# First feed-forward projection of a hybrid decoder: weights stationary against activations stationary

## The chip, the cores and the metric

The kernel runs on one core of a Trainium2 chip. A core has five engines that run their own instruction streams: TensorE (PE in the profile; PEld is its loading of stationary operands), VectorE (DVE), ScalarE (ACT), GpSimd (POOL) and SyncE (SP), which here only issues DMAs. The metric is the device time of one execution in microseconds (us), lower is better.

## The reference, cut to what matters

Two layers, 256 tokens, width 1024. Each layer is a half-step SwiGLU feed-forward network (FFN), a token mixing (windowed attention beside a diagonal state-space model, SSM), and a second FFN. All of it is float32.

```python
D_MODEL, SEQ, DEPTH, D_FF = 1024, 256, 2, 2816

def swiglu(h, w_in, w_out):
    a, b = jnp.split(h @ w_in, 2, axis=-1)
    return (jax.nn.silu(a) * b) @ w_out

for l in range(DEPTH):
    mod = (c_act @ w_ada[l] + b_ada[l]).reshape(Bsz, N_MOD, 1, D_MODEL)
    ...
    x = x + 0.5 * g1 * swiglu(modulate(rmsnorm(x, norm_ffn1[l]), sh1, sc1), w_ffn1_in[l], w_ffn1_out[l])
    x = x + g2 * mixing(modulate(rmsnorm(x, norm_mix[l]), sh2, sc2), ...)
    x = x + 0.5 * g3 * swiglu(modulate(rmsnorm(x, norm_ffn2[l]), sh3, sc3), w_ffn2_in[l], w_ffn2_out[l])
return rmsnorm(x, final_norm)
```

The SSM inside `mixing` needs, for each of 16 tiles of states in a layer, a table of the cosine and sine of the state's angle over the 256 tokens.

## The kernel before

The program is six sublayers in a row: FFN (sublayer 0), mixing (1), FFN (2), FFN (3), mixing (4), FFN (5). Activations lie with features on the 128 partitions and the 256 tokens along the free dimension: 8 chunks of 128 features, each split into a high float32r part (`hh`) and the rest (`hl`).

**Weights.** They arrive from HBM in units of 1 MB (`raw`, four buffers, DMAs issued by SP). Each unit is cut into two halves of 1024 columns. `split_one` splits a half: ACT casts it to `whi` (L163), DVE subtracts to get `wlo` (L164). Seven halves are in flight (`NHB`). `look`, called at each `half()`, splits as far ahead as buffers allow, so that the casts stand in ACT's stream some six halves ahead of the matmuls that read them. Among the weight units come units of the modulation's weights (`wada`), which DVE alone multiplies and sums (`ada_unit`, L247).

**First projection of an FFN** (`ffn_sub`). The 2816 gated columns are 22 tiles of 128; a loop over 11 pairs `p` makes, for each pair, two tiles of `a` (g = 0) and two of `b` (g = 1). A tile is one half of weights: 8 chunks times the three products of `mm3` (L201 to L203), each with a 128x128 block of weights stationary and 256 tokens moving. So a pair is 4 halves and 96 matmuls. Then ACT makes Silu (L843), DVE the product (L845), ACT and DVE split it in two (`split_act`, L340 and L341). The result has features on partitions, as the second projection (`fo`, 8 x 22 tiles) needs it. The first tiles of the stage come from `first_sublayer` (8 tiles, sublayer 0) or `first_block` (6 tiles, elsewhere).

**Tables beside it.** In sublayers 0 and 2, `side` holds a generator `table_side` that makes the 16 tables of the layer. Each `tick()` takes one step of it: first 12 (sublayer 0) or 8 (sublayer 2) empty steps, then 32 real ones, by turns "angles of state tile s" (`tp` and `tq` on ACT, L509 and L510, then four operations on POOL: L389, L387, L392, L392) and "cosine and sine of state tile s - 2" (`tb` on ACT, L525 to L527, then a DMA that POOL issues, L528). `tp` has three buffers, `tq` two, so `tq` of state tile s waits until POOL is done with s - 2, and `tb` of s - 2 waits for the same. The loop over pairs calls `tick` three times in a pair.

**Order.** ACT, POOL and SP run in the order in which the code emits; the order on PE and DVE is made by a scheduler when the kernel is built. Every engine runs its stream in order.

Of the kernel before, what the change touches and what calls it, by code (L numbers as in the profile page):

```python
# [58 lines left out]
NZ = 6  # L59
NATIVE = ()  # L60
# [3 lines left out]
def plan_units():  # L64
    """Order in which the units of weights are read: ('w', i) or ('a', i)."""
# [37 lines left out]
def trunk(ctx, tc, xT, cv, par, ssmp, cst, emat, tbl, wada, wpk, bmat, cmat, out):  # L103
# [37 lines left out]
    def take_ada():  # L141
        """Modulation units whose turn it is."""
# [42 lines left out]
    def several(n):  # L185
        """Halves that are read together."""
# [13 lines left out]
    def mm3(ps, wh, wl, hh, hl, start, stop):  # L200
        T.matmul(ps, lhsT=wh, rhs=hl, start=start, stop=False)  # L201
        T.matmul(ps, lhsT=wh, rhs=hh, start=False, stop=False)  # L202
        T.matmul(ps, lhsT=wl, rhs=hh, start=False, stop=stop)  # L203
# [31 lines left out]
    def ada_unit():  # L235
        """256 columns of silu(c) @ w_ada, one column per partition and element."""
# [57 lines left out]
    def soon(fn):  # L294
        """fn, with its instructions ahead of those that are emitted up to SOON earlier."""
# [16 lines left out]
    def rstd_start():  # L312
        """1 / sqrt(mean of squares + eps), tokens on partitions."""
# [17 lines left out]
    def rstd_spread(ys):  # L331
        """The same on every partition, in PSUM."""
# [10 lines left out]
    def h_tiles(r, scale, shift, hh, hl):  # L343
        """scale * x * r + shift in two parts, chunk by chunk; the chunks take turns in how much of it
        the scalar engine does."""
# [9 lines left out]
        for k in range(KC):  # L355
            hh.append(base.tile([128, S], F32R, name=f"hh{k}", tag=f"hh{k}"))
            hl.append(base.tile([128, S], F32R, name=f"hl{k}", tag=f"hl{k}"))
            b = shift[:, k:k + 1]
            if k % 2:
                A.activation(out=hh[k], in_=t, func=AF.Identity, bias=b)  # L360
            else:
                A.activation(out=t, in_=t, func=AF.Identity, scale=scale[:, k:k + 1], bias=b)
                A.copy(out=hh[k], in_=t)
            n = first(k + 1) if k + 1 < KC else None
            if k % 2:
                stt(hl[k], t, b, hh[k], AD, SU)
            else:
                tt(hl[k], t, hh[k], SU)
# [133 lines left out]
    def table_side(l, pool):  # L502
        """Cosine and sine of each state's angle over time, for the scans of layer l."""
# [27 lines left out]
    def gate_of(sub):  # L531
        """Half the gate."""
# [71 lines left out]
    def first_block(nx, sj, rj):  # L604
        """Five column tiles of a sublayer's input projection. They read scale * x; the rest read the
        normed chunks, which are made meanwhile. What comes back: the banks, 1 / rms, the normed chunks."""
# [5 lines left out]
        def mm(j, w, k):  # L612
            mm3(pss[j][:, :S + 2], w[0][:, k, :], w[1][:, k, :], z[:, k, 0, :], z[:, k, 1, :], k == 0, k == KC - 1)

        hh, hl = [], []
# [13 lines left out]
        for j in range(4):  # L629
            for k in range(5, KC):  # L630
                mm(j, hs[j], k)
            if j == rj:
# [3 lines left out]
                ht = h_tiles(rs, scale, shift, hh, hl)  # L636
# [12 lines left out]
        return pss, rs, hh, hl  # L649

    def first_block_whole(nx, sub):
        """The same for four column tiles, in plain float32."""
        scale, shift, z = nx
        us = [("w", first[sub] + j) for j in range(2)]
        ws = [raw.pop(u).rearrange("p (a b) -> p a b", b=128) for u in us]
        look()
        pss = [bank("b1") for _ in range(4)]

        def mms(ks):
            for j in range(4):  # L660
                for k in ks:
                    T.matmul(pss[j][:, :S + 2], lhsT=ws[j // 2][:, 8 * (j % 2) + k, :], rhs=z[:, k, :],
                             start=k == 0, stop=k == KC - 1)
                if ks[0] == 0 and j == 1:
                    stat_mm()
                    stat["ys"] = rstd_start()
                if ks[0] > 0 and j % 2:
                    finish(us[j // 2])
                    take_ada()

        mms(range(5))
        rps = rstd_spread(stat["ys"])
        rs = tmp.tile([128, S], F32, name="rs", tag="sqa", bufs=1)
        A.copy(out=rs, in_=rps)
        hh, hl = [], []
        for k in h_tiles(rs, scale, shift, hh, hl):
            pass
        mms(range(5, KC))
        look()
        return pss, rs, hh, hl  # L680
# [39 lines left out]
        # bias of each head by distance, for each kind of block of keys: [pq + pk] is that of query  # L720
        # 127 - pq and key pk of the block
# [661 lines left out]
```

## Time and profile before

| | us |
|---|---|
| median of 3 runs (lowest, highest) | 1365.01 (1364.72, 1365.94) |
| span of the profiled execution | 1361.8 |
| PE busy | 1322.1 (97%) |
| DVE busy | 1098.3 (81%) |
| ACT busy | 757.2 (56%) |
| POOL busy | 292.6 (21%) |

The profile is of one execution, whose span runs from its first to its last instruction; what lies around it in that execution is not listed; the median of the three runs is 3.2 us above the span. Matmuls overlap, so that PE's busy share says that it always had one in flight, not that it ran at its peak: how fast it goes is the distance between the starts of two matmuls. Idle time of an engine counts only where PE waits for it.

The first projections stand, in the profiled execution, at 52.8 to 170.3 us (sublayer 0), 528.3 to 636.6 (2), 717.3 to 825.5 (3) and 1180.2 to 1288.4 (5).

### The profile page before, as it was taken

How to read it: one execution, taken by the hardware profiler on the slowest of the kernel's cores; microseconds unless marked ns; L12 is line 12 of the kernel's file. 1: busy time of each engine (PE TensorE's matmuls, PEld its weight loads, DVE VectorE, ACT ScalarE, POOL GpSimd, SP SyncE). 2: the span in 40 equal slices, each digit the busy share in tenths (PEclk: the TensorE clock that was granted, in tenths of full speed). 3: DMA queues.
4: the chain of work that ended last, by engine and by line, in shares of the span. 5: the costliest groups of instructions: out<-in, count | busy, mean ns of one | idle time of the engine just before them, and what ended most of it. 6: DMA issues, size and time to landing. Idle time of an engine off the chain costs nothing.

```text
span 1361.8 us, 26855 instructions
## 1 busy us (share of the span) xinstructions
PE 1322.1 (97%) x11018; PEld 1279.4 (94%) x11018; DVE 1098.3 (81%) x1757; ACT 757.2 (56%) x1162; POOL 292.6 (21%) x356
## 2 busy tenths in 40 slices
PE   4996999999999999999999999999999999999997
PEld 2996999998988999999999999999889999999997
DVE  8866997889899879998769888679889887876552
ACT  5634795645565456677646444454565645654441
POOL 5889691100000000877300000010000000000000
PEclk9997999999999999999999999999999999999999
DMA  9775997556665645998837988656555463586540
GB/s 356 297 289 175 369 347 274 187 193 207 219 234 219 217 153 170 347 370 321 279 124 291 351 316 333 247 174 227 173 199 198 163 220 128 182 307 217 186 155 32
DMA packets 48837, 321.60 MB, mean 236 GB/s; under 512 B 6048, under 2 KB 6432, under 8 KB 12746
## 3 DMA queue, kind: packets, MB, share of 16 engines
q1 hardware_dynamic: 41704, 296.24, 59.8%
q0 software_dynamic: 7008, 23.64, 5.4%
q8 instruction: 86, 1.41, 0.4%
q14 instruction: 37, 0.30, 0.1%
q10 hardware_dynamic: 2, 0.00, 0.0%
HBM read 310.38 MB, written 9.48 MB: 235 GB/s over the span
## 4 chain that ended last, share of the span: by engine, by line
PE 86%; POOL 6%; DVE 3%; issue 2%; ACT 1%; DMA 1%; DVEq 0%; POOLq 0%; ACTq 0%
PE pc L203 8%; PE pc L201 8%; PE pc L202 8%; PE fo L201 6%; PE fo L202 6%; PE fo L203 6%; PE qk L201 4%; PE qk L202 3%; PE qk L203 3%; PE gt L201 3%; PE gt L202 2%; PE gt L203 2%; PE b L201 2%; PE bu L949 2%; PE b L203 2%; PE b L202 2%
## 5 line engine op out<-in xcount | busy, mean ns | idle before, releaser
L164 DVE TENSOR_TENSOR wlo<-raw,whi 128x1024 fp32r<-128x1024 f32 x416 | 515.5, 1257 | 93.2 <-ACT whi L163 92.3
L163 ACT CAST whi<-raw 128x1024 fp32r<-128x1024 f32 x416 | 427.0, 1047 | 220.2 <-PE fo L202 71.3
L201 PE MATMUL pc<-hl,whi 128*128 128x256 f32 x1200 | 338.4, 282 | 8.7 <-ACT whi L163 8.7
L203 PE MATMUL pc<-hh,wlo 128*128 128x256 f32 x1200 | 338.2, 282 | 3.6 <-DVE wlo L164 3.6
L202 PE MATMUL pc<-hh,whi 128*128 128x256 f32 x1200 | 338.2, 282 | 0.0
L201 PEld LDWEIGHTS pc<-hl,whi 128*128 128x128 f32 x1200 | 226.6, 189 | 8.9 <-ACT whi L163 8.9
L203 PEld LDWEIGHTS pc<-hh,wlo 128*128 128x128 f32 x1200 | 226.5, 189 | 4.1 <-DVE wlo L164 4.1
L202 PEld LDWEIGHTS pc<-hh,whi 128*128 128x128 f32 x1200 | 226.7, 189 | 0.0
L201 PE MATMUL fo<-al,whi 128*128 128x256 f32 x704 | 197.7, 281 | 0.2 <-DVE al L341 0.2
L202 PE MATMUL fo<-ah,whi 128*128 128x256 f32 x704 | 197.8, 281 | 0.0
L203 PE MATMUL fo<-ah,wlo 128*128 128x256 f32 x704 | 197.7, 281 | 0.0
L247 DVE CUSTOM_DVE_ANT_0 raw<-raw,cb 128x1024 f32<-128x1024 f32 x144 | 182.2, 1300 | 7.4 <-DMA raw<-wada 7.1
L201 PEld LDWEIGHTS fo<-al,whi 128*128 128x128 f32 x704 | 132.6, 188 | 0.4 <-DVE al L341 0.4
L202 PEld LDWEIGHTS fo<-ah,whi 128*128 128x128 f32 x704 | 132.7, 188 | 0.0
L203 PEld LDWEIGHTS fo<-ah,wlo 128*128 128x128 f32 x704 | 132.7, 188 | 0.0
L201 PE MATMUL qk<-hl,whi 128*128 128x256 f32 x352 | 102.4, 292 | 0.0
L202 PE MATMUL qk<-hh,whi 128*128 128x256 f32 x352 | 99.1, 282 | 0.0
L203 PE MATMUL qk<-hh,wlo 128*128 128x256 f32 x352 | 98.7, 281 | 0.0
L389 POOL TENSOR_SCALAR tr<-tp 128x256 f32<-128x256 f32 x32 | 45.6, 1424 | 146.8 <-ACT tp L509 146.1
L883 POOL DMA_DIRECT2D tab<-tab x32 | 17.4, 545 | 267.8 <-DVE pq L276 171.3
L201 PE MATMUL gt<-hl,whi 128*128 128x256 f32 x256 | 74.7, 292 | 0.0
L201 PEld LDWEIGHTS qk<-hl,whi 128*128 128x128 f32 x352 | 66.1, 188 | 7.1 <-issue 4.7
(220 smaller groups left out, 2915.4 us busy)
## 6 DMA issues: line engine op xcount, KB each, us to landing
raw<-wpk SPq DMA_DIRECT2D x208, 1024.0 KB, 5.4
raw<-wada SPq DMA_DIRECT2D x72, 1024.0 KB, 6.8
tab<-tb POOLq DMA_DIRECT2D x32, 256.0 KB, 5.7
tab<-tab POOLq DMA_DIRECT2D x32, 256.0 KB, 3.6
bt<-wd POOLq DMA_DIRECT2D x8, 640.0 KB, 6.2
xt<-xT SPq DMA_DIRECT2D x1, 1024.0 KB, 4.9
bT<-bmat POOLq DMA_DIRECT2D x2, 512.0 KB, 4.8
out<-xt SPq DMA_DIRECT2D x4, 256.0 KB, 2.2
```

The costliest lines, as they stand in the source:

```text
L163: A.copy(out=hi.rearrange("p a b -> p (a b)"), in_=src)
L164: low.tensor_sub(out=lo.rearrange("p a b -> p (a b)"), in0=src, in1=hi.rearrange("p a b -> p (a b)"))
L201: T.matmul(ps, lhsT=wh, rhs=hl, start=start, stop=False)
L202: T.matmul(ps, lhsT=wh, rhs=hh, start=False, stop=False)
L203: T.matmul(ps, lhsT=wl, rhs=hh, start=False, stop=stop)
L247: V.tensor_tensor_reduce(out=wj, in0=wj, in1=cb, scale=1.0, scalar=0.0, op0=ALU.mult, op1=ALU.add, accum_out=m[:, c:c + 1])
L389: G.tensor_scalar(out=o, in0=i, scalar1=s1, scalar2=s2, op0=op0, op1=op1)
L883: G.dma_start(out=tabs[s], in_=tabd[l][s])
L949: T.matmul(ps[:, i * S:i * S + S], lhsT=w[r, i, q, :], rhs=u[q][r], start=n == 0, stop=n == 2, tile_position=(32 * jj, 0))
```

## The change

In pairs 2 to 10 of each FFN's first projection (the pairs up to `OLD` = 2 stay as they were) the operands change places: a chunk of activations, 128 tokens, is stationary, and 512 columns of weights (two tiles of `a`, two of `b`) move. Result tiles have tokens on the partitions, one bank of PSUM for each half of the tokens. Silu and product are made on 256 columns for each half of the tokens; four PE transposes for a pair turn the product back, and the split reads the transposed product from PSUM. The transposes of a pair are emitted after the next pair's matmuls. The weights are packed on the host so that a half now holds two chunks of all 512 columns. `block512` calls `tick` after each of its four halves, and the loop once more: five calls in a pair. High and low parts of an activation now share a tile (`hx`, `ax`).

```diff
+    def mmt(ps, x, t, wh, wl, start, stop):
+        sl = slice(128 * t, 128 * t + 128)
+        T.matmul(ps, lhsT=x[:, 0, sl], rhs=wh, start=start, stop=False)
+        T.matmul(ps, lhsT=x[:, 1, sl], rhs=wh, start=False, stop=False)
+        T.matmul(ps, lhsT=x[:, 1, sl], rhs=wl, start=False, stop=stop)
+
+    def block512(name, x, n, tock):
+        ps = [bank(name) for t in range(2)]
+        for h in range(n // 2):
+            wh, wl = (w.rearrange("p (a b) c -> p a (b c)", a=2) for w in half())
+            for t in range(2):
+                for k in (2 * h, 2 * h + 1):
+                    mmt(ps[t], x[k], t, wh[:, k % 2], wl[:, k % 2], k == 0, k == n - 1)
+            tock()
+        return ps
...
+        def turned():
+            p, mu = waiting.pop(0)
+            pt = bank("pt").rearrange("p (j s) -> p j s", j=2)
+            for j in range(2):
+                for t in range(2):
+                    T.transpose(pt[:, j, 128 * t:128 * t + 128], mu[:, t, 128 * j:128 * j + 128], ident)
+            split_act(pt, ax[2 * p][0][:, :, 1], ax[2 * p][0][:, :, 0])
+
+        waiting = []
         for p in range(FC // 2):
...
+            if p >= OLD:
+                ps = block512("pc", hx, KC, tick)
+                for t in range(2):
+                    A.activation(out=sl[:, t], in_=ps[t][:, :S], func=AF.Silu)
+                    V.tensor_mul(out=mu[:, t], in0=sl[:, t], in1=ps[t][:, S:])
+                if waiting:
+                    turned()
+                waiting.append((p, mu))
+                tick()
+                continue
             for g in range(2):
...
-                    ps, rough = column(q, j, p < FC // 2 - 1 or g == 0)
+                    ps, rough = column(q, j, True)
...
             tick()
-            split_act(flat(mu), flat(a), flat(b))
+            split_act(mu, a[:, :, 1], a[:, :, 0])
+        turned()
...
     def ffn(w_in, w_out):
         t = tiles(w_in)
         for p in range(FC // 2):
-            for half in range(2):
-                for j in range(2):
-                    cols(t, half * FC + 2 * p + j)
+            if p < OLD:
+                for half in range(2):
+                    for j in range(2):
+                        cols(t, half * FC + 2 * p + j)
+            else:
+                for k in range(KC):
+                    for half in range(2):
+                        seq.append(t[k, half * FC + 2 * p:half * FC + 2 * p + 2])
```

The order on two engines, at the places that the prediction speaks of. ACT in sublayer 0 of the kernel before, from the Silu of pair 4 (`sl_1056`) over the first six steps of the tables (`tp`, `tq` of three state tiles) to the next cast (`whi` are casts of weights, `ah4` is the split of pair 4):

```order
L843 ACTIVATE sl_1056<-pc_1060 128x512
L509 ACTIVATE tp_1124<-cs_71,fhi_97 128x256
L510 ACTIVATE tq_1125<-cs_71,flo_98 128x256
L163 CAST whi_1134<-raw_1023 128x1024
L163 CAST whi_1162<-raw_1023 128x1024
L509 ACTIVATE tp_1197<-cs_71,fhi_97 128x256
L510 ACTIVATE tq_1198<-cs_71,flo_98 128x256
L509 ACTIVATE tp_1206<-cs_71,fhi_97 128x256
L510 ACTIVATE tq_1207<-cs_71,flo_98 128x256
L340 CAST ah4_1058<-mu_1057 128x512
L163 CAST whi_1222<-raw_1093 128x1024
```

The same place of the kernel after, where the tables begin behind the Silu of pair 2 (`sl_765`) and the Silu of pair 3 is `sl_862`:

```order
L840 ACTIVATE sl_765<-pc_769 128x256
L164 CAST whi_867<-raw_778 128x1024
L164 CAST whi_883<-raw_778 128x1024
L543 ACTIVATE tp_906<-cs_71,fhi_97 128x256
L544 ACTIVATE tq_907<-cs_71,flo_98 128x256
L164 CAST whi_915<-raw_810 128x1024
L543 ACTIVATE tp_931<-cs_71,fhi_97 128x256
L544 ACTIVATE tq_932<-cs_71,flo_98 128x256
L164 CAST whi_940<-raw_810 128x1024
L543 ACTIVATE tp_962<-cs_71,fhi_97 128x256
L544 ACTIVATE tq_963<-cs_71,flo_98 128x256
L840 ACTIVATE sl_862<-pc_865 128x256
```

The third `tq`, the first that needs a buffer back from POOL, stood behind the 26th half of weights (`whi_1162`) and stands behind the 22nd (`whi_940`) now, and a Silu is the next thing behind it.

PE in the kernel after, at the end of pair 4's matmuls (`pc_991`); `pt_1100` are the transposes of pair 3's product `mu_863`, `pc_1119` is pair 5:

```order
L217 MATMUL pc_991<-wlo_884,hx7_531 128x512
L828 MATMUL pt_1100<-cs_71,mu_863 128x128 x4
L215 MATMUL pc_1119<-whi_915,hx0_283 128x512
L216 MATMUL pc_1119<-whi_915,hx0_283 128x512
L217 MATMUL pc_1119<-wlo_916,hx0_283 128x512
```

In the kernel before no matmul of a first projection read a Silu; now the matmuls of pair 5 stand behind transposes that need the Silu of pair 3 and its product.

ACT in the kernel after, sublayer 0, from the last step of the tables (`tb_1692`) over the Silu of pair 9 (`sl_1620`) to that of pair 10 (`sl_1726`):

```order
L561 ACTIVATE tb_1692<-tb_1692,cpi_94 128x512
L164 CAST whi_1697<-raw_1577 128x1024
L840 ACTIVATE sl_1620<-pc_1623 128x256
L840 ACTIVATE sl_1620<-pc_1624 128x256
L371 CAST ax8_1493<-pt_1719 128x2x256
L164 CAST whi_1731<-raw_1581 128x1024
L164 CAST whi_1747<-raw_1581 128x1024
L164 CAST whi_1765<-raw_1650 128x1024
L164 CAST whi_1781<-raw_1650 128x1024
L840 ACTIVATE sl_1726<-pc_1729 128x256
L840 ACTIVATE sl_1726<-pc_1730 128x256
```

In the kernel before, the last steps of the tables stood among the casts of the second projection; now all of them stand ahead of the Silu of pair 9.

## Rows read from the trace of the kernel before

**Rows 1.** Page, engines: busy us, share of the span, instructions.

```profile
PE 1322.1 (97%) x11018; PEld 1279.4 (94%) x11018; DVE 1098.3 (81%) x1757; ACT 757.2 (56%) x1162; POOL 292.6 (21%) x356
```

**Rows 2.** Engines by stretch: PE, PEld, DVE, ACT, POOL busy (instructions); clock, DMA, GB/s.

```profile
53.00:170.00 117.00, 104.63 (x862) 103.93 (x862) 89.75 (x109) 64.40 (x100) 97.28 (x141) 0.94 0.73 270
528.00:636.00 108.00, 108.00 (x913) 108.00 (x912) 104.02 (x129) 79.17 (x127) 70.99 (x60) 1.00 0.89 333
717.00:825.00 108.00, 108.00 (x912) 108.00 (x911) 93.83 (x134) 51.65 (x62) 0.00 (x0) 1.00 0.85 319
1180.00:1288.00 108.00, 108.00 (x912) 108.00 (x912) 73.78 (x93) 53.74 (x66) 0.00 (x0) 1.00 0.67 243
```

**Rows 3.** PE in order of time: start us, us, instruction, idle before it.

```profile
112.99 0.58 PE L201 MATMUL pc<-hl,whi 128*128 128x256 f32 x1 [8.73 <-ACT whi L163]
...
117.43 0.58 PE L203 MATMUL pc<-hh,wlo 128*128 128x256 f32 x1 [3.64 <-DVE wlo L164]
...
118.24 0.41 PE L203 MATMUL pc<-hh,wlo 128*128 128x256 f32 x1
118.45 0.41 PE L201 MATMUL pc<-hl,whi 128*128 128x256 f32 x1
...
170.29 0.28 PE L201 MATMUL fo<-al,whi 128*128 128x256 f32 x1
...
636.55 0.28 PE L201 MATMUL fo<-al,whi 128*128 128x256 f32 x1
```

**Rows 4.** ACT by line, 53 to 170 us: instructions, busy, mean ns, idle before.

```profile
L163 ACT CAST whi<-raw 128x1024 fp32r<-128x1024 f32 x36 | 35.8, 1045 | 7.1 <-DMA raw<-wpk 5.9 <-PE pc L202 1.0
L527 ACT ACTIVATE tb<-tb,cpi 128x512 f32<-128x512 f32 x8 | 5.8, 725 | 0.3
L510 ACT ACTIVATE tq<-cs,flo 128x256 f32<-128x256 f32 x10 | 5.0, 498 | 24.8 <-POOL tp L392 20.1 <-POOL flo L387 4.7
L526 ACT ACTIVATE tb<-tp,cpi 128x256 f32<-128x256 f32 x8 | 4.0, 496 | 0.0
L525 ACT ACTIVATE tb<-tp 128x256 f32<-128x256 f32 x8 | 3.2, 406 | 0.0
```

**Rows 5.** POOL in order of time: a state tile's four operations and its DMA issue.

```profile
107.30 1.10 POOL L389 TENSOR_SCALAR tr<-tp 128x256 f32<-128x256 f32 x1
110.91 1.08 POOL L389 TENSOR_SCALAR tr<-tp 128x256 f32<-128x256 f32 x1
...
178.89 1.53 POOL L389 TENSOR_SCALAR tr<-tp 128x256 f32<-128x256 f32 x1
184.36 0.61 POOL L528 DMA_DIRECT2D tab<-tb  x1
185.00 1.44 POOL L389 TENSOR_SCALAR tr<-tp 128x256 f32<-128x256 f32 x1
...
547.41 1.28 POOL L389 TENSOR_SCALAR tr<-tp 128x256 f32<-128x256 f32 x1 [126.42 <-ACT tp L509]
```

**Rows 6.** Engines by stretch, columns as in rows 2.

```profile
70.00:93.00 23.00, 23.00 (x196) 23.00 (x195) 18.80 (x25) 9.80 (x14) 20.70 (x31) 1.00 0.83 309
93.00:107.00 14.00, 11.26 (x95) 11.05 (x94) 1.32 (x4) 0.00 (x0) 11.17 (x41) 1.00 0.39 151
118.00:170.00 52.00, 52.00 (x428) 51.81 (x427) 49.64 (x58) 35.21 (x60) 39.90 (x37) 0.97 0.93 347
```

**Rows 7.** PE in order of time, mixing: four transposes of 128 columns, one matmul behind.

```profile
389.07 0.60 PE L1050 MATMUL pt<-cs,lg 128*128 128x128 f32 x4
389.43 0.37 PE L201 MATMUL gt<-hl,whi 128*128 128x256 f32 x1
389.64 0.60 PE L1050 MATMUL pt<-cs,lg 128*128 128x128 f32 x4
```

**Rows 8.** DVE by line, 118 to 170 us, columns as in rows 4.

```profile
L164 DVE TENSOR_TENSOR wlo<-raw,whi 128x1024 fp32r<-128x1024 f32 x18 | 24.7, 1401 | 0.9 <-ACT whi L163 0.9
L247 DVE CUSTOM_DVE_ANT_0 raw<-raw,cb 128x1024 f32<-128x1024 f32 x14 | 20.0, 1466 | 0.0
```

More of the change, by code (lines that the diff above doesn't have):

```diff
@@ L59 @@
 NZ = 6
+OLD = 2
 NATIVE = ()
@@ L198, in wtile, with mm3, mm2, mmz @@
         return cur[0][0][:, k, :], cur[0][1][:, k, :]
[L200 to L203, printed above, removed]
+    def mm3(ps, wh, wl, x, start, stop):
+        T.matmul(ps, lhsT=wh, rhs=x[:, 0], start=start, stop=False)
+        T.matmul(ps, lhsT=wh, rhs=x[:, 1], start=False, stop=False)
+        T.matmul(ps, lhsT=wl, rhs=x[:, 1], start=False, stop=stop)
+    def mm2(ps, wh, wl, x, start, stop):
+        T.matmul(ps, lhsT=wh, rhs=x.rearrange("p a b -> p (a b)"), start=start, stop=False)
+        T.matmul(ps[:, :S], lhsT=wl, rhs=x[:, 1], start=False, stop=stop)
+    def mmt(ps, x, t, wh, wl, start, stop):
[12 more added lines that the diff above has]
+        return ps
+    def mmz(ps, wh, wl, z, start, stop):
+        T.matmul(ps, lhsT=wh, rhs=z[:, 1], start=start, stop=False)
+        T.matmul(ps, lhsT=wh, rhs=z[:, 0], start=False, stop=False)
+        T.matmul(ps, lhsT=wl, rhs=z[:, 0], start=False, stop=stop)
     cs = base.tile([128, 385], F32, name="cs")
@@ L341, in split_act, with part_tile, h_tiles @@
         V.tensor_sub(out=lo, in0=src, in1=hi)
-    def h_tiles(r, scale, shift, hh, hl):
+    def part_tile(k):
+        return base.tile([128, 2, S], F32R, name=f"hx{k}", tag=f"hx{k}")
+    def h_tiles(r, scale, shift, hx):
         def first(k):
@@ L648, in first_block @@
             split_one()
[L649 to L680, printed above, removed]
+        return pss, rs, hx
     def first_sublayer():
@@ L730, in first_sublayer @@
         pss = [bank("b1") for _ in range(BOOT)]
-        hh, hl, late = [], [], []
+        hx, late = [], []
         def low():
             if late:
-                hl.append(base.tile([128, S], F32R, name=f"hl{len(hl)}", tag=f"hl{len(hl)}"))
-                tt(hl[-1], late.pop(0), hh[len(hl) - 1], SU)
+                x, t = late.pop(0)
+                tt(x[:, 0], t, x[:, 1], SU)
         def mms(k):
             for j in range(BOOT):
-                T.matmul(pss[j][:, :S], lhsT=hs[j][0][:, k, :], rhs=hh[k], start=k == 0, stop=False)
-                T.matmul(pss[j][:, :S], lhsT=hs[j][1][:, k, :], rhs=hh[k], start=False, stop=False)
+                T.matmul(pss[j][:, :S], lhsT=hs[j][0][:, k, :], rhs=hx[k][:, 1], start=k == 0, stop=False)
+                T.matmul(pss[j][:, :S], lhsT=hs[j][1][:, k, :], rhs=hx[k][:, 1], start=False, stop=False)
             for j in range(BOOT):
-                T.matmul(pss[j][:, :S], lhsT=hs[j][0][:, k, :], rhs=hl[k], start=False, stop=k == KC - 1)
+                T.matmul(pss[j][:, :S], lhsT=hs[j][0][:, k, :], rhs=hx[k][:, 0], start=False, stop=k == KC - 1)
         for k in range(KC):
@@ L753, in first_sublayer @@
             t = boot.tile([128, S], F32, name="hb", tag="hb", bufs=2)
-            a = base.tile([128, S], F32R, name=f"hh{k}", tag=f"hh{k}")
+            hx.append(part_tile(k))
             A.activation(out=t, in_=xr[:, k, :], func=AF.Identity, scale=sc[:, k:k + 1], bias=sh[:, k:k + 1])
-            A.copy(out=a, in_=t)
-            hh.append(a)
-            late.append(t)
+            A.copy(out=hx[k][:, 1], in_=t)
+            late.append((hx[k], t))
             if k == 0:
@@ L822, in ffn_sub @@
             mu = fp.tile([128, 2, S], F32, name="mu", tag="mu", bufs=2)
-            a = fp.tile([128, 2, S], F32R, name=f"ah{p}")
-            b = fp.tile([128, 2, S], F32R, name=f"al{p}")
+            a = fp.tile([128, 2, 2, S], F32R, name=f"ax{p}")
+            ax += [(a, a[:, 0]), (a, a[:, 1])]
+            if p >= OLD:
[8 more added lines that the diff above has]
+                continue
             for g in range(2):
@@ L847, in ffn_sub @@
             tick()
-            split_act(flat(mu), flat(a), flat(b))
-            ah += [a[:, 0], a[:, 1]]
-            al += [b[:, 0], b[:, 1]]
+            split_act(mu, a[:, :, 1], a[:, :, 0])
+        turned()
+        ax = [x for _, x in ax]
         gate = gate_of(sub)
@@ L947, in ssm_in @@
                 for i in range(2):
-                    for n, (w, u) in enumerate(((bh, ul), (bh, uh), (bl, uh))):
-                        T.matmul(ps[:, i * S:i * S + S], lhsT=w[r, i, q, :], rhs=u[q][r], start=n == 0, stop=n == 2,
+                    for n, (w, u) in enumerate(((bh, 0), (bh, 1), (bl, 1))):
+                        T.matmul(ps[:, i * S:i * S + S], lhsT=w[r, i, q, :], rhs=ux[q][r, u], start=n == 0, stop=n == 2,
                                  tile_position=(32 * jj, 0))
@@ L1112, in v_quad @@
                             sl = slice(128 * tt_, 128 * tt_ + 128)
-                            T.matmul(o, lhsT=hl[k][:, sl], rhs=wh, start=k == 0, stop=False)
-                            T.matmul(o, lhsT=hh[k][:, sl], rhs=wh, start=False, stop=False)
-                            T.matmul(o, lhsT=hh[k][:, sl], rhs=wl, start=False, stop=k == KC - 1)
+                            T.matmul(o, lhsT=hx[k][:, 0, sl], rhs=wh, start=k == 0, stop=False)
+                            T.matmul(o, lhsT=hx[k][:, 1, sl], rhs=wh, start=False, stop=False)
+                            T.matmul(o, lhsT=hx[k][:, 1, sl], rhs=wl, start=False, stop=k == KC - 1)
                         tock()
```

81 lines of the change are left out of this document (37 added, 44 removed).

## The prediction

> **What bounds the kernel now.** I read the page's table of engines first, then the busy times by stretch, then the order of time around every gap of PE. The engines: PE is busy 97% of the span, so what is to be won is won in the pace of its matmuls, and what is to be lost is a wait that PE does not have yet [rows 1]. The stretches: in the first projections of sublayers 2, 3 and 5 PE never rests, 912 or 913 matmuls in 108 us, which is 118.4 ns from start to start [rows 2]. Sublayer 0 is the exception: 104.63 of 117 us, with POOL busy 97.28 [rows 2]. In order of time, PE stands there for 8.73 us until 112.99 because no cast comes from ACT, and 3.64 us more until 117.43 [rows 3]. The waits by line say why ACT was late: `tq` waited 20.1 us for POOL's last operation on a table and 4.7 us for `flo`, a parameter that POOL computes [rows 4]. POOL, still busy with the SSM's parameters, starts its first table at 107.30 [rows 5]. So the thing to look at beside PE's pace is the chain POOL, ACT, PE: ACT runs its stream in order, and a table step that waits for POOL holds up every cast and every Silu behind it.
>
> **The change part by part.**
>
> *Matmuls.* A pair loses 96 matmuls of 256 columns, 96 x 0.1184 = 11.37 us, and gets 48 of 512. No row has a 512-column float32r matmul. Upper bound: twice the 256-column one, 0.237. Lower bound: at half the clock the 256 columns are 0.21 us apart (118.24 to 118.45) [rows 3]; that is the columns alone, since twice as many columns at full clock take the same 0.21, so the lower bound is 0.213. The 12 ns by which the 256-column matmul at full clock (0.1184) exceeds half of that do not show once a matmul lasts 0.21 us. I take 0.215, next to the lower row: 48 x 0.215 = 10.32.
>
> *Transposes.* Four in a pair. In the mixing four of them and one matmul take 389.07 to 389.64, 0.57 us [rows 7]; less 0.12 for the matmul, 0.45. The Trainium skill, page "TensorE: Matmul & The Clock Gate", section "Part 4: PE-mode transpose", gives about 275 ns for one in a kernel's context. The trace disagrees: 0.11 us each in a row of four. By the page's figure a pair would pay 1.1 us instead of 0.45, and the change could not gain on PE at all (estimate: 36 pairs x 0.65 = 23 us, spread over four sublayers, half of it hidden under the waits below).
>
> *PE's balance.* 11.37 - 10.32 - 0.45 = 0.60 us for a pair, 5.4 us for the nine pairs of a sublayer. The last pair's turn was covered before by 20 of 22 tiles of the second projection; now its first transpose stands ahead of that projection. Half of the tokens is finished six matmuls (1.3 us) before the other, and its Silu and product take some 0.4 us each (ACT's 256-column passes take 0.41 to 0.50 [rows 4]), so this wait is short: 0 to 3 us, I take 1. The extra fixed cost of two Silus and two products on ACT and DVE lies under 10.8 us of PE, where DVE has 14 to 34 us free in a stage and ACT more (the last two of [rows 2]). Sublayers 3 and 5, which have no tables: -4.4 each, -9 together. Bounds: 0.237 for the matmul makes a pair 0.45 slower, +4 + 1 each, +10.
>
> *Ticks.* This is the part that decides. The tables take 32 steps in either kernel, but the loop calls five in a pair instead of three. A state tile is two steps: 1.5 state tiles in a pair before, 2.5 now. So ACT asks POOL for one in 10.77 / 2.5 = 4.3 us. POOL needs 178.89 to 185.00 = 6.1 us for one while DVE is busy, and 107.30 to 110.91 = 3.6, with 0.61 for the DMA issue 4.2, while DVE rests [rows 5]. Before, the demand was one in 11.37 / 1.5 = 7.6 us, so POOL kept up. Now it does not, and behind the waiting `tq` and `tb` ACT's stream holds casts and Silus, and behind the Silu of pair p PE's stream holds the transposes of p and all of pair p + 2 (the order in the part on the change). The casts run ahead, but PE can't pass the transposes: its lead on ACT is one pair.
>
> How long is a state tile then? DVE works 49.64 us in 52 [rows 6], in which PE ran 428 matmuls or 4.5 pairs: 11 us for a pair. At 2.5 x 5.7 = 14.25 us for a pair DVE is 77% busy, and 4.2 + 0.77 x (6.1 - 4.2) = 5.7: consistent. I take 5.7, bounds 4.2 and 6.2. Half the clock, which PE shows after its waits in the stage now (0.21 us apart until some 3 us after 117.43 [rows 3]), would take its 1 to 2 us out of the 3.5 us that PE then waits in each pair.
>
> *Sublayer 0.* The third `tq` comes four halves earlier and waits for POOL's parameters as before. From then on no casts come, so DVE rests and POOL is quicker: it did 31 operations in 20.7 busy us at 70 to 93 and 41 in 11.17 at 93 to 107, when DVE worked 1.32 us [rows 6]. Before, ACT stopped 20.1 us ahead of 110.91, at 90.8 [rows 4, 5]; now it stops some eight us (three halves of PE's time, which free its buffers) behind pair 2, whose matmuls run from 52.8 to about 64, at 72, so that some 27 of those 31 take 0.27 instead of 0.67: 10 us sooner, the first table at 97.5. Sixteen state tiles x 5.7 = 91 later, at 188.5, POOL is done; ACT makes the last cosine and sine, 0.41 + 0.50 + 0.73, a cast of 1.05 and the Silus of pair 9: 192. Then four casts (4.2), the Silus of pair 10, its product and transposes, some 2 us more: the second projection starts at about 198 instead of 170.29 [rows 3, 4]. +28; at 5.2 and 6.2 us for a state tile +20 and +36.
>
> *Sublayer 2.* The first step lies in pair 2 as before, so POOL starts at 547.41 again [rows 5]; 16 x 5.7 brings it to 638.6. The last step stands ahead of the Silu of pair 8: +3.1 as above, product and transposes 0.9, then pair 10's matmuls, 10.3, and the tail of 2: 655 instead of 636.55 [rows 3]. +19; at 5.2 and 6.2 +11 and +27.
>
> *The rest.* Packing, joint tiles for high and low parts and the first blocks leave the same instructions, DMAs and queues: 0.
>
> **Sum.** 28 + 19 - 9 = +38 on the span of 1361.8 makes 1399.8; with the 3.2 us between span and median, 1403.
>
> **The rivals.**
>
> *The tables hide (ends faster).* If POOL makes a state tile in 4.3 us or less, it never holds ACT. For it: 4.2 us while DVE rests, and that the split of a pair now reads PSUM and not two tiles of SBUF. Against it: DVE has as much to do as before. Then sublayer 0: PE goes on at about 101.5 with six pairs of 10.77 and loses 2 us to half the clock and the tail, 168 against 170.3, so -2; sublayer 2 -4.4; 1365 - 2 - 4.4 - 9 = 1350. The point from which this decides is a state tile of about 4.7 us.
>
> *512 columns cost twice 256.* The tables bind as forecast, and sublayers 3 and 5 cost 10 instead of gaining 9: 1403 + 19 = 1422. For it: the 12 ns might be paid for each 256 columns; against it the spacing at half clock [rows 3].
>
> *POOL and DVE exclude each other wholly.* If POOL's work can't overlap DVE's passes over two operands in SBUF, a pair costs their sum: `wlo` and `ada`, 24.7 + 20.0 us for 4.5 pairs [rows 8], 9.9 for a pair, and 2.5 x 3.4 for POOL, 18.4 in all, 7.4 for a state tile. Sublayers 0 and 2 then cost 27 more each: 1457. Against it: at 118 to 170 POOL made eight state tiles, 27 us of quiet work, beside those 44.7, together more than the 52 there are. It is the rule of the Trainium skill, page "SBUF — State Buffer", section "SBUF: two separate sides", that the pair of ports that these two share is locked for a whole instruction. The trace agrees in kind, since POOL's operations stretch while DVE works, and not in size.
>
> **How the numbers follow.** Forecast 0.67, hidden tables 0.08, 512 at twice the price 0.18, full exclusion 0.07. The forecast's own range is 1387 to 1419 (5.2 to 6.2 us for a state tile). The range for 8 in 10 leaves out most of the first and last rival: 1374 to 1436. About 0.2% is what a measurement of this kernel tells from no change. Faster 0.08, from the first rival; same 0.02, from a state tile near 4.7 us; slower 0.90.
>
> **What would show it.** In sublayers 3 and 5, matmuls of 512 columns 0.215 us apart and the second projection starting some 4 us sooner after the first block. In 0 and 2, POOL without a gap through its 16 state tiles, ACT waiting before `tq` or `tb` for POOL's last operation in nearly each, PE waiting before each `pt` of a pair for the product, and tables that end before the second projection starts. I am wrong if PE's first projections in 0 and 2 stay without such waits, or if POOL's state tiles come 4.3 us apart.

## The result, and the profile after

The changed kernel takes 1427.26 us (1425.62 to 1428.89, four runs) against 1364.87 (1363.96 to 1365.94): a ratio of 1.0455, 95% interval 1.0441 to 1.047. The forecast was 1403, its own range 1387 to 1419, the range for 8 in 10 1374 to 1436. So the sign and the wide range held; the time lies 8 us above the forecast's own range, and the forecast came out 24 us short.

The page's engines after, against [rows 1]: 1584 matmuls fewer and PE at 94% instead of 97% of a span that is 62.7 us longer.

```profile
PE 1344.1 (94%) x9434; PEld 1216.1 (85%) x9434; DVE 1095.2 (77%) x1793; ACT 763.1 (54%) x1198; POOL 282.7 (20%) x356
```

The first projections of sublayers 0, 2, 3 and 5, one row each (columns as in [rows 2]):

```profile
53.00:202.00 149.00, 113.88 (x468) 89.31 (x466) 100.20 (x122) 86.28 (x152) 126.36 (x176) 0.88 0.68 246
562.00:694.00 132.00, 114.78 (x513) 92.14 (x513) 105.56 (x139) 89.84 (x155) 89.63 (x80) 0.95 0.80 288
776.00:885.00 109.00, 109.00 (x510) 89.78 (x509) 96.28 (x143) 54.37 (x71) 0.00 (x0) 1.00 0.84 321
1240.00:1350.00 110.00, 110.00 (x518) 90.69 (x517) 76.77 (x105) 57.54 (x76) 0.00 (x0) 1.00 0.65 238
```

PE rests 35 us in sublayer 0 and 17 in sublayer 2, where it had rested 12 and 0, and the mean granted clock there is lower, 0.88 and 0.95 instead of 0.94 and 1.00. Where there are no tables (sublayers 3 and 5) PE never rests, and the stage is still 1.5 and 1.3 us longer than before. The third number of the lines below is the longest wait; the first three are of 53 to 203 us, the other two of 562 to 695, in the waits by line:

```profile
PE pt L828 <- DVE mu L841: 35.2, 7, 17.1
ACT tb L559 <- DMA tab<-tb: 25.5, 10, 6.0
ACT tq L544 <- POOL tp L426: 21.8, 2, 20.1
...
ACT tb L559 <- DMA tab<-tb: 27.7, 10, 5.8
...
PE pt L828 <- DVE mu L841: 15.9, 4, 6.0
```

PE waits at the transposes, as the order said it must. One of its waits in sublayer 0, the 17.1 us that end at 104.45, is for the first tables; the other 18 us come later. ACT waits for POOL's first tables and, in 20 waits at `tb`, for the DMA that carries off a finished table. POOL in order of time is what [rows 5] were before: it starts its first table at 99.49 and ends its last operation at 189.2, 5.6 us for each of 16 state tiles; in sublayer 2, which begins 34 us later now, at 579.99 and 672.3, 5.8 each. In the first stretch no gap between two of its instructions, DMA issues included, is over 0.1 us until 188.4, nor in the second until 671.2. So POOL sets the pace of the tables, although ACT's waits mostly end with a DMA: POOL issues these DMAs too, behind the operations of a later state tile.

```profile
99.49 1.10 POOL L423 TENSOR_SCALAR tr<-tp 128x256 f32<-128x256 f32 x1
103.10 1.08 POOL L423 TENSOR_SCALAR tr<-tp 128x256 f32<-128x256 f32 x1
107.58 2.06 POOL L423 TENSOR_SCALAR tr<-tp 128x256 f32<-128x256 f32 x1
...
184.68 1.97 POOL L423 TENSOR_SCALAR tr<-tp 128x256 f32<-128x256 f32 x1
...
188.49 0.73 POOL L426 TENSOR_TENSOR tp<-tp,tq 128x256 f32<-128x256 f32 x1
...
579.99 1.23 POOL L423 TENSOR_SCALAR tr<-tp 128x256 f32<-128x256 f32 x1 [125.57 <-ACT tp L543]
```

PE in sublayer 3, a quiet stretch: 512-column matmuls 0.23 us apart, then a pair's transposes.

```profile
802.84 0.40 PE L216 MATMUL pc<-whi,hx 128*128 128x512 f32 x1
803.07 0.39 PE L217 MATMUL pc<-wlo,hx 128*128 128x512 f32 x1
803.30 0.39 PE L215 MATMUL pc<-whi,hx 128*128 128x512 f32 x1
803.53 0.39 PE L216 MATMUL pc<-whi,hx 128*128 128x512 f32 x1
803.76 0.39 PE L217 MATMUL pc<-wlo,hx 128*128 128x512 f32 x1
803.99 0.60 PE L828 MATMUL pt<-cs,mu 128*128 128x128 f32 x4
804.35 0.48 PE L215 MATMUL pc<-whi,hx 128*128 128x512 f32 x1
```

Over the 415 intervals between neighbours in the stage the mean is 0.2322; most lie between 0.228 and 0.233, one in eight between 0.240 and 0.242. (The first interval behind a pair's transposes is often 0.316; it counts to the transposes.)

### The profile page after: what moved, and what is told of

Its sections match the earlier page's. It is cut to its first block, busy times and chain, and to the rows that moved or that the text cites. A ratio compares the mean times of both kernels' runs of the same rounds, so it can differ in the third digit from the quotient of the medians.

```text
span 1424.5 us, 23802 instructions
## 1 busy us (share of the span) xinstructions
PE 1344.1 (94%) x9434; PEld 1216.1 (85%) x9434; DVE 1095.2 (77%) x1793; ACT 763.1 (54%) x1198; POOL 282.7 (20%) x356
## 4 chain that ended last, share of the span: by engine, by line
PE 76%; POOL 17%; DMA 2%; DVE 2%; issue 2%; ACT 1%; POOLq 0%; DVEq 0%; ACTq 0%
PE fo L204 6%; PE fo L203 6%; PE fo L205 6%; POOL tp L426 5%; PE pc L216 5%; PE pc L215 5%; PE pc L217 5%; PE qk L203 3%; POOL tr L423 3%; PE qk L204 3%; PE qk L205 3%; PE gt L203 2%; POOL tr L421 2%; PE gt L204 2%; PE gt L205 2%; PE bu L969 2%
## 5 line engine op out<-in xcount | busy, mean ns | idle before, releaser
L215 PE MATMUL pc<-whi,hx 128*128 128x512 f32 x576 | 233.9, 406 | 0.0
L216 PE MATMUL pc<-whi,hx 128*128 128x512 f32 x576 | 231.7, 402 | 0.0
L217 PE MATMUL pc<-wlo,hx 128*128 128x512 f32 x576 | 227.0, 401 | 1.9 <-DVE wlo L165 1.9
L203 PE MATMUL fo<-ax,whi 128*128 128x256 f32 x704 | 199.3, 283 | 0.0
L204 PE MATMUL fo<-ax,whi 128*128 128x256 f32 x704 | 198.8, 282 | 0.0
L205 PE MATMUL fo<-ax,wlo 128*128 128x256 f32 x704 | 198.7, 282 | 0.0
L217 PEld LDWEIGHTS pc<-wlo,hx 128*128 128x128 f32 x576 | 110.9, 193 | 28.7 <-DVE wlo L165 3.2
L203 PEld LDWEIGHTS fo<-ax,whi 128*128 128x128 f32 x704 | 133.8, 190 | 0.0
L204 PEld LDWEIGHTS fo<-ax,whi 128*128 128x128 f32 x704 | 133.7, 190 | 0.0
L205 PEld LDWEIGHTS fo<-ax,wlo 128*128 128x128 f32 x704 | 133.6, 190 | 0.0
L215 PEld LDWEIGHTS pc<-whi,hx 128*128 128x128 f32 x576 | 111.8, 194 | 24.9 <-ACT whi L164 0.4
L216 PEld LDWEIGHTS pc<-whi,hx 128*128 128x128 f32 x576 | 111.0, 193 | 24.0
L203 PE MATMUL qk<-hx,whi 128*128 128x256 f32 x352 | 102.4, 292 | 0.0
L204 PE MATMUL qk<-hx,whi 128*128 128x256 f32 x352 | 99.1, 282 | 0.0
L203 PE MATMUL gt<-hx,whi 128*128 128x256 f32 x256 | 74.7, 292 | 0.0
L204 PE MATMUL gt<-hx,whi 128*128 128x256 f32 x256 | 72.2, 282 | 0.0
```

What stands on the lines that cost most here:

```text
L203: T.matmul(ps, lhsT=wh, rhs=x[:, 0], start=start, stop=False)
L204: T.matmul(ps, lhsT=wh, rhs=x[:, 1], start=False, stop=False)
L205: T.matmul(ps, lhsT=wl, rhs=x[:, 1], start=False, stop=stop)
L215: T.matmul(ps, lhsT=x[:, 0, sl], rhs=wh, start=start, stop=False)
L216: T.matmul(ps, lhsT=x[:, 1, sl], rhs=wh, start=False, stop=False)
L217: T.matmul(ps, lhsT=x[:, 1, sl], rhs=wl, start=False, stop=stop)
```

## The experiments

All times from the first matmul of a first projection to the first of the second one, in the profiled executions, us:

| kernel | median | sublayer 0 | 2 | 3 | 5 |
|---|---|---|---|---|---|
| before | 1364.9 to 1365.6 | 117.5 | 108.2 | 108.2 | 108.2 |
| after | 1427.3 | 149.4 | 132.3 | 109.7 | 109.6 |
| after, three steps | 1378.1 | 123.9 | 109.7 | 109.7 | 109.6 |
| before, five steps | 1411.2 | 140.5 | 123.7 | 108.2 | 108.2 |
| after, not turned | 1401.3 | 141.0 | 124.4 | 106.1 | 106.1 |
| after, three steps, not turned | 1360.0 | 113.8 | 106.1 | 106.1 | 106.1 |
| after, short POOL | 1391.6 | 131.4 | 114.7 | 109.7 | 109.6 |
| before, tables 4 steps later | 1357.4 | 113.1 | 108.2 | 108.2 | 108.2 |
| after, three steps, tables 4 later | 1371.8 | 118.1 | 109.7 | 109.7 | 109.6 |
| before, tables 10 later | 1351.5 | 102.5 | 108.2 | 108.2 | 108.2 |
| after, three steps, tables 10 later | 1362.3 | 108.6 | 109.7 | 109.7 | 109.6 |

The theory: the loss is the tables' pace, five steps in a pair. The rival: it is the transposes, which tie PE to the Silus. The figures behind a time are its ratio to the kernel before and the ratio's 95% interval.

**Three steps in the changed kernel.**

```diff
-            tock()
+            if h % 2:
+                tock()
```

> The changed kernel with three table steps in a pair instead of five (after the second half, after the fourth, and at the end of the pair). Theory, the pace of the tables: the loss of sublayers 0 and 2 goes, what is left is the longer matmul, about 0.2 us for each of nine pairs in four sublayers, so 1365 + 4 x 1.5 = 1371, at most 1378 with waits for the transposes; the second projections of sublayers 0 and 2 start within 6 us of where they started before. Rival, the transposes themselves: PE cannot pass them, so a late Silu costs PE time whatever the number of steps; the time stays above 1405.

1378.13 (1.0092, 1.0078 to 1.0106): 49 of the 62 us come back, sublayer 2 entirely but for 1.5, what sublayers 3 and 5 lose too. The time lies just above the theory's upper end, because sublayer 0 keeps 6.4 where 6 were allowed: PE waits there 7.3 us for a cast, since ACT waits 19.2 us for the first tables behind POOL's parameters as before, and 7.2 for products. In sublayer 0 fewer steps also move the first table, to 106.84 us, so the pace alone shows in sublayer 2, where POOL starts 18.8 us into the stage and started 17.4 us into it with five steps.

```profile
ACT tq L545 <- POOL tp L427: 19.2, 1, 19.2
...
PE pc L215 <- ACT whi L164: 7.3, 1, 7.3
PE pt L829 <- DVE mu L842: 7.2, 2, 3.6
```

**Five steps in the kernel before.** The other way about: the suspected cost alone, with no change of operands.

```diff
                 for j in range(2):
                     ps, rough = column(q, j, ...)
+                    if p >= 2:
+                        tick()
...
-                tick()
+                if p < 2:
+                    tick()
```

> The kernel before with five table steps in a pair instead of three, nothing else (weights stationary, no transposes). Theory, the pace of the tables: ACT's stream stops behind POOL and with it the casts, so sublayers 0 and 2 get slower by 15 to 30 us each: 1395 to 1425. Rival, the transposes: without them PE runs on over the waits of ACT, 1365 to 1372.

1411.23 (1.0342, 1.0327 to 1.0358): the theory. Without any transposes PE stands all the same, now in front of the weights. The waits of 53 to 194 us, ACT's first:

```profile
ACT tb L525 <- DMA tab<-tb: 25.3, 9, 4.2
...
ACT tq L510 <- POOL tp L392: 21.1, 2, 19.8
...
PE pc L201 <- ACT whi L163: 16.2, 2, 13.9
...
PE pc L203 <- DVE wlo L164: 13.5, 5, 5.0
```

**The changed kernel without the transposes,** with five and with three steps; the operands are changed as before.

```diff
-            pt = bank("pt").rearrange(...)
-            for j in range(2):
-                for t in range(2):
-                    T.transpose(...)
-            split_act(pt, ...)
+            split_act(mu, ...)
```

> The changed kernel, five table steps, without the four transposes of a pair: the split reads the product as it lies, tokens on partitions, so the output is another one. PE then reads no Silu in a first projection. Theory, the pace of the tables with the transposes as an addition: the kernel before with five steps lost 46 us without them, and 48 matmuls of 0.232 are 0.22 us shorter than 96 of 0.1184, 8 us less in all: about 1403 (1398 to 1410), the rest of the changed kernel's loss being the transposes, 16 us of their own time and 5 to 8 of waits. Rival, ACT's order alone (a Silu or cast held by a table step) makes the whole loss and the transposes only add their own time: 1427 - 16 = 1411 or more.

> The changed kernel with three table steps in a pair and without the transposes (the product is not turned, so the output is another one). What is left of the change is the operands alone. Theory: 36 pairs x 0.44 us of transposes and the waits in front of them go, 1378 - 16 - 5 = 1357 (1354 to 1361); sublayers 3 and 5 go from 109.6 us to 106, two below the kernel before. Rival, the transposes lie in time that PE loses anyway: 1375 or more, sublayers 3 and 5 at 109.

1401.31 (1.0266, 1.0251 to 1.0281) and 1359.99 (0.9964, 0.995 to 0.9978): the theory both times. With five steps sublayers 0 and 2 take nearly the same as the kernel before with five steps (141.0 and 124.4 against 140.5 and 123.7). With three steps sublayers 3 and 5, where PE never rests, show the prices: the operands alone gain 2.2 us in a sublayer, and the transposes take back 3.5 or 3.6 there and 0.4 in the second projection: 4.0 for nine pairs, 0.45 us a pair. With five steps the transposes cost 1427 - 1401 = 26 us in all, so the waits that they add to the tables' are 26 - 4 x 4.0 = some 10 us, against the 5 to 8 expected. PE's stretch of sublayer 3 without transposes:

```profile
715.00:820.00 105.00, 105.00 (x476) 86.14 (x475) 93.50 (x138) 53.58 (x71) 0.00 (x0) 1.00 0.86 327
```

48 of the 476 matmuls are of 256 columns (two tiles of pair 1) and take 5.7 us; the other 428 have 99.3, 0.232 each, the same as with transposes.

**POOL's operations on 64 columns.**

```diff
-            gts(b, p, -0.125, AD, MAGIC, AD)
+            n = slice(0, 64)
+            gts(b[:, n], p[:, n], -0.125, AD, MAGIC, AD)
...
```

> The changed kernel, five steps, with POOL's four operations of a state tile on 64 of 256 columns (the tables' other columns stay unreduced, so the output is another one); ACT's steps and the DMAs stay. Theory, POOL's pace: a state tile takes under 3 us, less than the 4.3 that five steps ask for, and the loss of sublayers 0 and 2 goes as with three steps: 1372 to 1384. Rival, what holds ACT is the number of steps in its own stream, or the DMA that frees the tables' buffers: 1410 or more.

1391.57 (1.0189, 1.0173 to 1.0205) lies between the two, in neither range. 36 of the 62 us go, so POOL's pace is the larger part of the loss. But sublayer 2 stays 5 us longer than with three steps. There POOL no longer works without a gap (its gaps add up to 10 us between 561 and 637), and ACT still waits for the tables' DMA, half as long as before (544 to 659 us):

```profile
ACT tb L560 <- DMA tab<-tb: 14.0, 6, 4.7
```

So a second limit seems to stand behind POOL: two buffers for finished tables, and 5 to 7 us from issue to landing; no run gives five steps a third buffer, which would show it. The first line is of the page after, the second of this kernel:

```profile
tab<-tb POOLq DMA_DIRECT2D x32, 256.0 KB, 5.3
```

```profile
tab<-tb POOLq DMA_DIRECT2D x32, 256.0 KB, 6.7
```

The operations did not become four times shorter either. Two of one kind, one behind the other, take 0.33 and 1.35 us here, a spread like that of the SSM's small operations (last section):

```profile
605.98 0.33 POOL L426 TENSOR_TENSOR tp<-tp,tr 128x64 f32<-128x64 f32 x1
606.39 1.35 POOL L426 TENSOR_TENSOR tp<-tp,tq 128x64 f32<-128x64 f32 x1
```

**Tables later in sublayer 0.** The kernel before lost 8.7 and 3.6 us there already [rows 3]; this asks what each kernel is worth without that wait.

```diff
-            side.extend([None] * (12 if sub == 0 else 8) + ...)
+            side.extend([None] * (16 if sub == 0 else 8) + ...)
```

> The kernel before with sublayer 0's tables starting four steps later (16 empty steps instead of 12), so that ACT does not reach the first table step before POOL is done with its parameters. Theory: the waits of 8.7 and 3.6 us and the stretch at half the clock behind them go, 1365 - 12 = 1353 (1350 to 1358). Rival: the last tables move into the second projection and hold its casts, or POOL becomes free later as DVE goes on working beside it: 1362 to 1372.

> The changed kernel with three table steps in a pair and sublayer 0's tables starting four steps later: both disturbances taken out, what is left is the change of operands alone. Theory, the 512-column matmul costs 0.232 us: some 1.5 us more in each of four sublayers than the kernel before with later tables, about 1359 if that one gives 1353. Rival, the change of operands pays in itself once the tables are out of the way: 4 us less for each sublayer, 16 less than that kernel, about 1337.

1357.43 (0.9947, 0.9934 to 0.9959) and 1371.76 (1.0046, 1.0033 to 1.0059). The first lies in the theory's range, with part of its rival's mechanism: DVE goes on beside POOL, and the parameters are done at 118.24 instead of 107.30, so ACT still waits 16.62 us at its third `tq`, and later 8.51 for a table's DMA. In the kernel before with later tables:

```profile
104.82 0.50 ACT L509 ACTIVATE tp<-cs,fhi 128x256 f32<-128x256 f32 x1
121.94 0.51 ACT L510 ACTIVATE tq<-cs,flo 128x256 f32<-128x256 f32 x1 [16.62 <-POOL tp L392]
...
143.04 0.42 ACT L525 ACTIVATE tb<-tp 128x256 f32<-128x256 f32 x1 [8.51 <-DMA tab<-tb]
```

The second kernel came out 14.3 above the first where I expected 6; neither the theory's 1359 nor the rival's 1337. Its sublayer 0 takes 5.0 more, with PE 5.39, 0.80 and 5.28 us in front of transposes, and 2.1 more in the second projection. So the transposes do have a price in waits of their own, in sublayer 0.

**Later still, and a third buffer,** with three table steps instead of two for each tile of the second projection.

```diff
-                tab = pool.tile([128, 2, S], F32, name="tb", tag="tb", bufs=2)
+                tab = pool.tile([128, 2, S], F32, name="tb", tag="tb", bufs=3)
...
-            side.extend([None] * (12 if sub == 0 else 8) + ...)
+            side.extend([None] * (22 if sub == 0 else 8) + ...)
...
-                if k % 8 == 7:
+                if k % 7 == 6:
                     tick()
```

> The kernel before with sublayer 0's tables starting ten steps later (22 empty steps), three steps instead of two for each tile of the second projection so that they end with it, and a third buffer for a finished table. With four steps later ACT still waited for the parameters until 121.94 and 8.51 us for a table's DMA, and PE lost 2.07, 0.76, 3.0 and 0.8 us and half the clock behind them. Theory: these waits go too, sublayer 0's first projection takes the 108.3 us of the other three, 1357.4 - 5 = 1352.5 (1351 to 1355). Rival: the tables now hold the casts of the second projection of sublayer 0, where POOL has as much to do, 1358 to 1366.

> The changed kernel with all that helped the kernel before: three table steps in a pair, sublayer 0's tables ten steps later (22 empty steps), three steps for each tile of the second projection, a third buffer for a finished table. Theory, the change of operands with its transposes costs some 1.4 us in a first projection and 0.5 in the second projection behind it, in each of four sublayers, once no table holds it: 1351.5 + 8 = 1359 (1357 to 1362), a little below the kernel before and above the same kernel with weights stationary. Rival, the transposes meet waits in sublayer 0 in any case: 1364 or more.

1351.53 (0.9905, 0.9889 to 0.992) and 1362.30 (0.9976, 0.9966 to 0.9985), the latter a hair above the theory's range. The kernel before is the fastest of all with this: sublayer 0's first projection has no gap any more and full clock. Its 102.5 us, less than the 108.3 expected, are 864 matmuls at the others' pace; the other three stages have 912. What each of the three edits gave was not told apart.

```profile
53.00:155.00 102.00, 102.00 (x862) 102.00 (x862) 88.48 (x112) 57.22 (x80) 93.65 (x117) 1.00 0.83 308
```

The changed kernel with the same help stays 10.8 us behind it. 4.3 of them are one wait in front of the last pair's transposes, whose product stands in DVE's stream behind four subtractions and a modulation unit. PE, and DVE before it, in that kernel:

```profile
161.19 0.33 PE L829 MATMUL pt<-cs,mu 128*128 128x128 f32 x1 [4.28 <-DVE mu L842]
```

```profile
151.20 5.79 DVE L165 TENSOR_TENSOR wlo<-raw,whi 128x1024 fp32r<-128x1024 f32 x4
157.86 1.60 DVE L279 CUSTOM_DVE_ANT_0 raw<-raw,cb 128x1024 f32<-128x1024 f32 x1 [0.86 <-DMA raw<-wada]
...
159.39 1.40 DVE L279 CUSTOM_DVE_ANT_0 raw<-raw,cb 128x1024 f32<-128x1024 f32 x1
160.72 0.74 DVE L842 TENSOR_TENSOR mu<-sl,pc 128x256 f32<-128x256 f32 x2
```

The rest is 1.3 to 1.8 in a first projection and 0.4 in a second, four times: the change of operands with its transposes as such.

**What 512 columns cost.** Three kernels do none of the kernel's work: groups of matmuls, alone or with other engines and loads beside them, one execution each.

> Matmuls alone, in nine groups of 96 behind 40 to warm up, with all other engines and the DMAs at rest: float32r of 512 columns with the stationary operand changed each time, changed once in 48, and with the same moving operand; float32r of 256 columns with the stationary operand changed each time and once in 48; bfloat16 of 512 and of 256 columns; float32r of 128 and of 384 columns. None of the kernel's work is done. Theory, the price is the matmul's own and linear in its columns: 0.232 us for 512, 0.1185 for 256, 0.175 for 384, with changed and unchanged stationary operand alike. Rival, the change of the stationary operand costs: with an unchanged one 0.213 to 0.216. Rival, the other engines and DMAs slow it in the full kernel: 0.213 to 0.216 in all groups of 512. Rival, float32r: bfloat16 gives 0.213 to 0.216, float32r 0.232.

> Float32r matmuls of 512 columns in groups of 120, each with other company: alone, beside VectorE's subtractions of 1024 columns, beside ScalarE's copies of 1024 columns, beside loads of 1 MB from HBM, beside all three; then 240 of 256 columns beside all three, and 120 of 512 alone again. None of the kernel's work is done. Alone they were 0.2267 us apart in the run of spacings before, in the kernel 0.2322. Theory, company: one of the three, the loads most likely, brings 0.2267 to 0.232, and the 256 columns stay near 0.119. Rival, the kernel's own operands and stream (instructions, semaphores): 0.2267 in every group.

> Float32r matmuls of 512 columns with the changed kernel's own tiles and order (three products, weights in seven high and seven low tiles, activations in eight tiles of two parts, chains of 24 into changing banks), without readers of the banks and then with ScalarE reading them; then one of the three at a time: the activations' tiles as stationary operand, the high tiles as moving operand, high and low tiles by turns as moving operand; at last the kernel before's three products of 256 columns. None of the kernel's work is done. Theory, the kernel's operands: 0.232 us in the first groups, and one of the three single ones shows which, 256 columns at 0.1185. Rival, the kernel's stream (semaphores of many tiles, the other engines' work on the same tiles): 0.2267 in all, 256 columns at 0.120.

The rows by line, with first and last start. In the first run: 512 columns of float32r with a stationary operand changed each time, and once in 48; 256 columns, likewise; then 512 and 256 of bfloat16; 128 and 384 of float32r.

```profile
L135 PE MATMUL ps<-wr,xr x96: 389/389/390, 21.1 to 42.7; 128*128 128x512 f32 x96
L137 PE MATMUL ps<-wr,xr x96: 389/389/389, 42.9 to 64.4; 128*128 128x512 f32 x96
...
L141 PE MATMUL ps<-wr,xr x96: 277/283/283, 86.4 to 97.8; 128*128 128x256 f32 x96
L143 PE MATMUL ps<-wr,xr x96: 279/283/283, 97.9 to 109.3; 128*128 128x256 f32 x96
L145 PE MATMUL ps<-wb,xb x96: 379/379/390, 109.4 to 130.0; 128*128 128x512 bf16 x96
L147 PE MATMUL ps<-wb,xb x96: 272/273/273, 130.2 to 140.5; 128*128 128x256 bf16 x96
L149 PE MATMUL ps<-wr,xr x96: 272/275/306, 140.6 to 151.2; 128*128 128x128 f32 x96
L151 PE MATMUL ps<-wr,xr x96: 331/334/390, 151.3 to 167.9; 128*128 128x384 f32 x96
```

From start to start, by the mean of each group's 95 intervals: float32r 0.2267 for 512 columns, 0.1200 for 256, 0.174 for 384 and 0.112 for 128, bfloat16 0.2159 and 0.1092. Whether the stationary operand changes makes no difference at 512 and 256. So a float32r matmul has a fixed part of some 13 ns (twice 0.1200 less 0.2267; the 384 columns fit, the 128, which take 0.112, do not), and bfloat16 one of 2.5 (twice 0.1092 less 0.2159). In the second run the groups beside VectorE, ScalarE, the loads and all three were 0.2267 apart to the last digit, though the loads moved 238 GB/s; in the third, the changed kernel's own tiles, order and chains gave 0.2267 too, with and without readers, and the three products of 256 columns 0.1200. The theories of company and of the operands both fall. In the whole kernels the numbers are 0.2322 and 0.1186. What makes the 5.5 ns more (and the 1.4 less) there stays open: the many semaphores of their stream and the length of the busy stretch are in none of these runs.

## Why the prediction was right, and where it was too small

**The path (right).** ACT's stream held by POOL, and PE by ACT, was the forecast, and both directions show it: five steps alone cost the old kernel 46 us, three steps give the new one 49 back. The same arithmetic sized it: 2.5 state tiles in a pair at 4.3 us asked, 5.7 taken; measured 5.6 and 5.8. The first table's start stood at 97.5 in the forecast and at 99.49 in the trace, POOL's end in sublayer 0 at 188.5 and 189.2, in sublayer 2 at 638.6 and, in the old kernel's time, 638.1. Two of the signs named in advance came weaker than stated: ACT's waits at `tb` ended with a table's DMA and not with POOL's last operation, and PE waited in front of transposes 7 times in sublayer 0 and 4 times in sublayer 2, not in each of nine pairs.

**Sublayers 0 and 2 (too small by 5.8 and 5.5).** The second projections start 32.0 and 24.1 us later in their sublayers, not 28 and 19, with another 1.8 and 0.4 inside them. What was missing lies behind POOL's end. In sublayer 2 I gave ACT 3.1 us from there to the Silu of pair 8. It took 7.8, because ACT waited 5.80 us for the DMA that frees a table's buffer, a wait that the forecast left out altogether:

```profile
678.71 0.42 ACT L559 ACTIVATE tb<-tp 128x256 f32<-128x256 f32 x1 [5.80 <-DMA tab<-tb]
...
680.18 0.64 ACT L840 ACTIVATE sl<-pc 128x256 f32<-128x256 f32 x2
```

In sublayer 0 pair 10's Silus came at 199.81 instead of 196, its products only behind four subtractions on DVE, and PE had the last of the turn's inputs at 202.56:

```profile
197.55 4.62 DVE L165 TENSOR_TENSOR wlo<-raw,whi 128x1024 fp32r<-128x1024 f32 x4
202.09 0.41 DVE L841 TENSOR_TENSOR mu<-sl,pc 128x256 f32<-128x256 f32 x1
```

```profile
202.56 0.48 PE L828 MATMUL pt<-cs,mu 128*128 128x128 f32 x1 [4.57 <-DVE mu L841]
202.69 0.56 PE L203 MATMUL fo<-ax,whi 128*128 128x256 f32 x1
203.04 0.41 PE L204 MATMUL fo<-ax,whi 128*128 128x256 f32 x1
```

There PE is at half clock again (granted clock 0.50 from 202.6 to 206.8, 0.21 us for 256 columns): 1.4 of the 1.8 us inside the second projection; the other 0.4 are transposes, as in the other sublayers.

**PE's balance (wrong in sign).** The forecast gave sublayers 3 and 5 -4.4 us each; they take 1.5 and 1.3 more, and 0.4 more in the second projection. The step that failed is the lower bound of the matmul, "that is the columns alone", read from half clock, with the sentence that the 12 ns do not show once a matmul lasts 0.21 us. At full clock they do, at 512 columns too: at half clock a matmul has no visible fixed part (0.427 for 512 columns after PE's waits, twice the 0.213 for 256), at full clock and alone float32r has 13 ns at either width. One fixed part in place of two saves 13 ns for each two 256-column matmuls there, not the 22 taken; in the kernel it is 5 (twice 0.1186 less 0.2322). The Trainium skill, page "TensorE: Matmul & The Clock Gate", section "Wait — 56ns, not 53.3ns?", says just this of the two clocks: nothing fixed at 1.2 GHz, 2.5 ns in each matmul at 2.4. The bfloat16 rows agree with that figure, the float32r rows have five times as much. With 48 x 0.2322 + 0.45 = 11.60 against 11.37 a pair costs 0.23 us more, 2.0 for nine; 1.9 and 1.7 were measured. The transposes' 0.45 was right. The disagreement that the prediction saw in the trace was none, though: its 275 ns are the length of one transpose, and one lasts 0.272 us in the trace after (median of 144). Four in a row overlap and start 0.108 apart, and that spacing is the price.

**The rivals.** Hidden tables and full exclusion did not come: POOL's pace did not fall to 4.7 us and did not rise to 7.4. The rival "512 columns cost twice 256" was nearer to sublayers 3 and 5 than the forecast (+5 each by its price, about +2 measured, -4.4 forecast), and its 1422 is nearer to 1427; its price of 0.237 is still not reached.

The sum, measured: 33.8 + 24.5 + 1.9 + 1.7 = 61.9 for sublayers 0, 2, 3 and 5 with their second projections, of 62.7 in the span; forecast 28 + 19 - 9. Of the missing 24 us, half lies in sublayers 3 and 5, the matmul's price, and half in 0 and 2, most of it in the tails shown. Both errors point the same way, so neither hid the other.

## What to carry to other kernels

When a loop is rewritten, count what else it calls in each round: here two more calls of a side job in a pair cost 46 us by themselves, three quarters of the loss. A longer matmul saves one fixed part for each one that goes, so measure that part at full clock before the operands are swapped, and set the turn back against it: here 5 ns saved 48 times against 0.45 us. Before such a change, look for the wait that is there already: moving the tables behind POOL's parameters, with a third buffer and more steps later, gave 1% to the old kernel, more than the operands could have (0.4% without any transposes).

## What the runs showed of the hardware

- Float32r matmuls have a fixed part of about 13 ns each at full clock at 256, 384 and 512 columns (0.1200, 0.174, 0.2267 us apart), bfloat16 2.5 (0.1092 and 0.2159 for 256 and 512); at half clock 256 and 512 columns of float32r show none (0.213 and 0.427). VectorE and ScalarE at work and 238 GB/s of loads change nothing in it.
- POOL's pace hangs on DVE even for tiny operations: in the kernel before with later tables one on 128x32 took 0.25 to 0.3 us at 107 to 118 us, when DVE was busy 1.56 of 11, and mostly 1.0 to 1.2 at 93 to 107, when it was busy 12.75 of 14. So the SSM's parameters were done at 99, 107 or 118 us (after, before, before with later tables), the earlier the sooner DVE had been held up. It is DVE and not ACT, and not every instruction of DVE: in the kernel before with tables ten steps later, such operations (53 to 130 us) took 0.26 us on average beside ACT alone (11 of them) and 0.26 beside DVE's `mu`, which reads a bank of PSUM (11), but 0.34 beside the split's `al` (9), 0.91 beside `wlo` (22) and 1.13 beside the modulation's sums (9), which read SBUF alone.
- In the whole kernel 512 float32r columns took 0.2322 and 256 took 0.1186, alone 0.2267 and 0.1200; this was not explained.
